# Five pieces of work moved in a two-network transformer kernel: attention's start, two spectra, GpSimd work, and a late norm factor

## The chip, the cores and the metric

The kernel runs on one core of one Trainium2 chip. Its engines each execute their own list of instructions in order: TensorE (PE, with its weight loads PEld) multiplies, VectorE (DVE), ScalarE (ACT) and GpSimd (POOL) work on elements, and SyncE (SP) issues the loads of weights. They wait for one another by semaphores. The metric is the device time of one launch in microseconds (us); three launches of the kernel before took 2412.6, 2415.0 and 2419.7 us.

## The reference

Two stacked blocks act on 256 latent rows, the second one also on 256 context rows, all of width 1024 and in float32. What matters here is the second block, in two layers:

```python
def na_hyena_mixer(h_lat, h_ctx, ...):           # layer 0
    # 8 heads of attention, latent queries on latent (with a bias) and context keys
    a_lat = merge_heads(neighbourhood_attention(qk_norm(qa_l), qk_norm(ka_l), va_l, k_c, va_c, rpb))
    b_lat = hyena_operator(p_lat[..., 3 * NA_WIDTH:], conv_w, conv_b, filter_params, d_bias)
    o_lat = jnp.concatenate([a_lat, b_lat], axis=-1) @ w_out
    ...                                          # the same for the context rows
def hyena_operator(u, conv_w, conv_b, filter_params, d_bias):
    x0, x1, v = jnp.split(short_conv(u, conv_w, conv_b), 3, axis=-1)
    z = v * x1
    y = long_conv(z, filt) + z * d_bias          # long_conv: product of spectra
    return y * x0
def modulate_2(x, gain, shift, scale):
    return rms_norm(x, gain) * (1 + scale) + shift
def swiglu_2(h, w_in, w_out):
    a, b = jnp.split(h @ w_in, 2, axis=-1)
    return (jax.nn.silu(a) * b) @ w_out
```

Layer 1 has a retention mixer in the place of attention: four heads whose score matrices are multiplied by decay tables, sums of exp(log gamma x distance) for the forward and the backward scan. Every mixer and every network takes a modulated norm of the residual, and adds its gated output to it.

## The kernel before

Activations lie with the channel on the partitions: `r` is the residual (8 tiles of 128 channels, 256 latent columns and 256 context columns), `yH` and `yL` its modulated norm as a high and a low part. Each product is three matmuls of reduced-precision floats (`mm3`, L172 high x high, L173 low activation x high weight, L174 high x low weight; in the changed file these are L175 to L177). Weights come in tiles `wraw` of 128x1024 by SP, in four buffers; `cut` makes the high part `wH` by a cast on ACT (L149) and the low part `wL` by a subtraction on DVE (L150), or on POOL for the hyena weights `even_hy`. There are three buffers of each. Matmul results lie in four groups of PSUM banks, `mm`, `sc`, `tp` and `sm`, two banks each.

The order of instructions on each engine is set by a scheduler from the order of the program and its own costs, and is then fixed: an instruction that waits holds back all that stand behind it on its engine.

Five places matter.

1. The mixer of layer 0 first makes q, k and v (`proj_tm`), then the generator `attention()` and the convolutions `conv(n)` run interleaved; `seg` 1 stands for the context queries. The softmax scale of a tile is L984 on DVE, PE then transposes the scaled tile (`tp`, L574).
2. `spectrum(s)` transforms `z` by matmuls (L585), multiplies it by the filter's spectrum (L1062 to L1074), and `signal(s, Y)` transforms it back (L1083, `mm` banks). `spectrum(0)` stands behind the first of the last four convolutions; `spectrum(1)` is in `rest()`, which runs in pieces between the tiles of the output product `even_out`.
3. The retention mixer's tables `decL` and `decC`: exponentials on ACT (L1310, L1311), then 24 instructions of 128x384 on DVE (L1313 to L1316). The `sg` buffers, two of them, hold the intermediate exponentials and are also used by `turn_y` (L1182).
4. The class `Norm` collects squares of the residual tile by tile (`add`), makes the factor 1/rms (`finish`: L329 and L330 sum over channels, L332 a root on ACT, L334 to L340 on DVE, L343 spreads it), and `modulated` writes `yH` and `yL` (L357 to L359).
5. The last network `fb1` (`up`, L425 on) starts after `flush()`, which issues all that is left of `modulated`.

Of the kernel before, what the change touches and what calls it, by code (L numbers as in the profile page):

```python
# [27 lines left out]
NEARLY = 9  # L28
LEADS = (1, 1, 0, 0)
# [44 lines left out]
def trace(tc, A, dbg=None):  # L74
# [50 lines left out]
    yH = tl(const, [P, ND, 2 * T], F32R, "yH")  # L125
    yL = tl(const, [P, ND, 2 * T], F32R, "yL")
# [26 lines left out]
    class Feed:  # L153
# [4 lines left out]
        def next(self):  # L158
            out = ready.pop((self.w, self.i), None) or cut(load(A[self.w][self.i]), self.eng)
            self.i += 1  # L160
            return out
# [200 lines left out]

    class TwoNorms(Norm):
# [91 lines left out]
    def ffn_steps(hp, nslot, w_gu, w_dn, keys, gate_ch, segs, norms, lead=0, done=None, pre=None):  # L455
# [29 lines left out]
        for gi, (k0, k1) in enumerate(groups):  # L485
            last = gi == len(groups) - 1
            fs = list(range(k0, k1))
            if gi == 0 and lead:
                for f in fs[:lead]:
                    hidden(f)  # L490
                for i, q in enumerate(segs):
                    if i:
                        flush()
                    for f in fs[:lead]:
                        ups(f, [q])
                        tick(-(-ND // lead))
                        yield
                fs = fs[lead:]
            for f in fs:
                hidden(f)  # L500
                ups(f, segs[:1] if f in pre else segs)
                yield
            for q in segs:
                need(keys[q], gate_ch)
            for part in ([[q] for q in segs] if last else [segs]):
                feed = Feed(w_dn, k0)
                for d in range(ND):
                    ps = bank(tags[d % 2], [P, T * len(part)])
                    down(ps, feed, k0, k1, part)
                    resid_add(ps, d, part, keys, gate_ch, norms if last else None)  # L510
                    tick(1)
                    yield
                if last and done is not None:
                    flush()
                    for q in part:
                        done(q)

    def ffn(w_gu, w_dn, keys, gate_ch, segs, to, norms, done=None, lead=0, start=0.0, by=1.0, hook=None, pre=None,
            nslot=0):
        both = len(segs) == 2  # L520
        with ExitStack() as st:
            hp = pool("ffn_h", stack=st)
            steps = ffn_steps(hp, nslot or (12 if both or w_dn in GROUPED else 22), w_gu, w_dn, keys, gate_ch, segs, norms, lead, done, pre)
# [379 lines left out]
    with ExitStack() as st:  # L903
# [9 lines left out]
        lat, ctx_ = (0, 1), (2, 3)  # L913
        for i, (n, tiles) in enumerate(((0, lat), (1, lat), (0, ctx_), (1, ctx_), (2, ctx_), (2, lat))):
            out = proj_tm("even_qkv", n, tiles, ("mm", "mm") if i % 2 == 0 else ("sc", "sc"))
            tick(4)
            for ps, tt in zip(out, tiles):
                if n == 2:
                    act.copy(vt[:, tt, :], ps)
                    continue  # L920
                sq = tl(tpool, [P, 512], F32, "sg", 2)
                act.activation(sq, ps, AF.Square)
                ss = tl(spool, [P, 8], F32, "qss")
                vec.tensor_reduce(ss, sq.rearrange("p (h e) -> p h e", h=8), AX, OP.add)
                rs = mean_rsqrt(ss, 8, 64)
                vec.tensor_tensor(qkn[n][:, tt, :].rearrange("p (h e) -> p h e", h=8),
                                  ps.rearrange("p (h e) -> p h e", h=8),
                                  rs.rearrange("p (h o) -> p h o", o=1).to_broadcast([P, 8, 64]), op=OP.mult)

# [31 lines left out]
        def weights(h, seg):  # L961
# [4 lines left out]
            for qt in (2 * seg, 2 * seg + 1):  # L966
# [17 lines left out]
                vec.tensor_scalar(s[:, :nk], s[:, :nk], rin, None, op0=OP.mult)  # L984
# [47 lines left out]

        def conv(n, dst):
# [13 lines left out]
        def spectrum(s):  # L1047
# [19 lines left out]
            vec.tensor_tensor(zr, zr, specB, op=OP.mult)  # L1067
            for i in range(2):
                vec.tensor_tensor(zi[i], zi[i], specA[:, i, :], op=OP.mult)
                vec.tensor_tensor(zi[i], zi[i], zr[:, i, :], op=OP.add)  # L1070
# [26 lines left out]
        steps = attention()  # L1097
# [5 lines left out]
        run(steps, 1)  # L1103
        hyx0 = tl(mp, [P, 4, 512], F32, "qk2n0", 1)
        for c in range(4):
            conv(c, hyx0[:, c, :])
            if c == 0:
                Y = spectrum(0)
        run(steps, 100)
        signal(0, Y)  # L1110
        heads(0)

        def rest():

            Y = spectrum(1)
            yield
            heads(1)
            yield
            signal(1, Y)
            yield  # L1120
# [18 lines left out]
    with ExitStack() as st:  # L1139
# [162 lines left out]
        for dst, pairs in ((DL, (0, 4)), (DC, (2,))):  # L1302
# [5 lines left out]
            for h in range(4):  # L1308
# [3 lines left out]
                if len(tabs) == 2:  # L1312
                    vec.tensor_tensor(ef, ef, tabs[1][:, 0, :], op=OP.mult)  # L1313
                    vec.tensor_tensor(dst[:, h, :], dst[:, h, :], tabs[1][:, 1, :], op=OP.mult)
                vec.tensor_tensor(dst[:, h, :], dst[:, h, :], ef, op=OP.add)
                vec.tensor_scalar(dst[:, h, :], dst[:, h, :], 1.0 / 16.0, None, op0=OP.mult)  # L1316
# [20 lines left out]
        nm = [Norm(0)]  # L1337
# [3 lines left out]
    flush()  # L1341
    ffn("fb1_gu", "fb1_dn", kk1, 8, [0], len(units), None)
# [172 lines left out]
```

## Time and profile before

| | |
|---|---|
| three launches | 2412.6, 2415.0, 2419.7 us |
| the profiled launch | 2415.01 us, of which the span of its instructions is 2413.3 us |
| PE busy | 2367.9 us (98%) |
| DVE busy | 1730.2 us (72%) |
| ACT busy | 1029.8 us (43%) |
| POOL busy | 47.4 us (2%) |
| mean granted TensorE clock | 0.993 |

PE is busy nearly everywhere, so the time it is idle, or runs at a lower clock, is what a change of order can take away or add. Of a row of a timeline the first number is the start, the second the duration; a bracket behind it has the idle time of the engine just before and what ended it. In the table of stretches each stretch has its length, then busy time of PE, PEld, DVE, ACT and POOL with the number of instructions, the granted clock and the share of the DMA engines.

### The profile page before, as it was taken

What the parts mean: (1) busy time and instruction counts of PE and PEld (TensorE: products, weight loads), DVE (VectorE), ACT (ScalarE), POOL (GpSimd) and SP (SyncE); (2) the same over time, 40 slices, a digit from 0 to 9 for tenths busy, and PEclk for the clock granted to TensorE, in tenths of its full rate; (3) what the DMA queues carried; (4) which work ended last, traced back from release to release, by engine and by line L of the source; (5) the groups of instructions that cost most, each with busy time, mean ns of one, the idle gap of its engine ahead of it and who ended that gap; (6) DMA issues with size and microseconds to landing.
All of it is one profiled execution on the core that took longest, in us unless ns stands there. A gap on an engine that the chain in (4) does not pass through costs nothing.

```text
span 2413.3 us, 38351 instructions
## 1 busy us (share of the span) xinstructions
PE 2367.9 (98%) x15304; PEld 2127.8 (88%) x15304; DVE 1730.2 (72%) x3063; ACT 1029.8 (43%) x1549; POOL 47.4 (2%) x47
## 2 busy tenths in 40 slices
PE   7999999999999999998999999999999999999999
PEld 4999889999998888877988888998888988999999
DVE  6889987665998689789875556877454786565554
ACT  4444575444432236675632222542222563344442
POOL 0000000000000000230000000000000000000000
PEclk9999999999999999999999999999999999999999
DMA  8897865665674455411463434564444542244554
GB/s 317 318 311 249 310 219 170 207 214 207 226 243 170 151 192 195 157 62 55 158 218 131 157 140 149 175 210 175 175 175 165 186 154 96 97 135 147 193 186 145
DMA packets 124660, 442.75 MB, mean 183 GB/s; under 512 B 13984, under 2 KB 18208, under 8 KB 124352
## 3 DMA queue, kind: packets, MB, share of 16 engines
q1 hardware_dynamic: 123216, 436.30, 51.9%
q0 software_dynamic: 1120, 3.80, 0.5%
q8 instruction: 120, 1.97, 0.3%
q14 instruction: 60, 0.49, 0.1%
q10 hardware_dynamic: 144, 0.19, 0.0%
HBM read 439.19 MB, written 1.05 MB: 182 GB/s over the span
## 4 chain that ended last, share of the span: by engine, by line
PE 53%; DVE 2%; ACT 1%; issue 0%; ACTq 0%
PE mm L172 9%; PE mm L173 9%; PE mm L174 9%; PE sc L174 8%; PE sc L172 8%; PE sc L173 8%; PE tp L1227 1%; PE sm L172 1%; PE sm L173 1%; PE sm L174 1%; PE tp L574 1%; PE mm L1083 0%; ACT wH L149 0%; DVE wL L150 0%; PE sm L1008 0%
## 5 line engine op out<-in xcount | busy, mean ns | idle before, releaser
L149 ACT CAST wH<-wraw 128x1024 fp32r<-128x1024 f32 x598 | 626.3, 1049 | 1036.6 <-PE mm L173 374.6
L150 DVE TENSOR_TENSOR wL<-wraw,wH 128x1024 fp32r<-128x1024 f32 x586 | 716.2, 1224 | 346.5 <-ACT wH L149 336.5
L172 PE MATMUL mm<-yH,wH 128*128 128x256 f32 (+1 forms) x1736 | 553.4, 319 | 6.4 <-ACT wH L149 3.8
L174 PE MATMUL mm<-yH,wL 128*128 128x256 f32 (+1 forms) x1736 | 551.0, 317 | 3.5 <-DVE wL L150 3.5
L173 PE MATMUL mm<-yL,wH 128*128 128x256 f32 (+1 forms) x1736 | 551.5, 318 | 0.6 <-DVE yL L702 0.3
L174 PE MATMUL sc<-yH,wL 128*128 128x256 f32 (+1 forms) x1192 | 385.9, 324 | 5.7 <-DVE wL L150 5.5
L172 PE MATMUL sc<-yH,wH 128*128 128x256 f32 (+1 forms) x1192 | 387.0, 325 | 0.4 <-ACT wH L149 0.3
L173 PE MATMUL sc<-yL,wH 128*128 128x256 f32 (+1 forms) x1192 | 385.2, 323 | 0.0
L172 PEld LDWEIGHTS mm<-yH,wH 128*128 128x128 f32 x1736 | 328.7, 189 | 29.8 <-ACT wH L149 4.1
L174 PEld LDWEIGHTS mm<-yH,wL 128*128 128x128 f32 x1736 | 328.5, 189 | 26.7 <-DVE wL L150 4.2
L173 PEld LDWEIGHTS mm<-yL,wH 128*128 128x128 f32 x1736 | 328.5, 189 | 23.4 <-DVE yL L702 1.0
L270 DVE SCALAR_TENSOR_TENSOR mjunk<-mraw,crow_c 128x1024 bf16<-128x1024 f32 x200 | 244.2, 1221 | 26.6 <-DMA mraw<-in_wada_dram 15.2
L174 PEld LDWEIGHTS sc<-yH,wL 128*128 128x128 f32 x1192 | 225.5, 189 | 26.6 <-DVE wL L150 7.2
L172 PEld LDWEIGHTS sc<-yH,wH 128*128 128x128 f32 x1192 | 225.8, 189 | 20.8 <-ACT wH L149 1.0
L173 PEld LDWEIGHTS sc<-yL,wH 128*128 128x128 f32 x1192 | 225.6, 189 | 20.1 <-DVE yL L178 0.5
L174 PE MATMUL sc<-hH,wL 128*128 128x256 f32 (+1 forms) x636 | 191.9, 302 | 1.2 <-DVE wL L150 1.2
L172 PE MATMUL mm<-hH,wH 128*128 128x256 f32 (+1 forms) x636 | 192.9, 303 | 0.0
L173 PE MATMUL mm<-hL,wH 128*128 128x256 f32 (+1 forms) x636 | 192.4, 303 | 0.0
L172 PE MATMUL sc<-hH,wH 128*128 128x256 f32 (+1 forms) x636 | 192.2, 302 | 0.0
L174 PE MATMUL mm<-hH,wL 128*128 128x256 f32 (+1 forms) x636 | 191.9, 302 | 0.0
L173 PE MATMUL sc<-hL,wH 128*128 128x256 f32 (+1 forms) x636 | 191.8, 302 | 0.0
L270 DVE SCALAR_TENSOR_TENSOR mjunk<-mraw,crow_c_ctx 128x1024 bf16<-128x1024 f32 x112 | 137.0, 1223 | 4.5 <-ACT crow_c_ctx L224 2.5
(418 smaller groups left out, 3289.5 us busy)
## 6 DMA issues: line engine op xcount, KB each, us to landing
mraw<-in_wmod_dram SPq DMA_DIRECT2D x144, 512.0 KB, 4.6
wraw<-in_fa_gu_dram SPq DMA_DIRECT2D x116, 512.0 KB, 3.6
wraw<-in_fb_gu_dram SPq DMA_DIRECT2D x94, 512.0 KB, 3.3
wraw<-in_w_gu_dram SPq DMA_DIRECT2D x88, 512.0 KB, 4.0
wraw<-in_fa_dn_dram SPq DMA_DIRECT2D x60, 512.0 KB, 3.7
mraw<-in_wada_dram SPq DMA_DIRECT2D x56, 512.0 KB, 5.4
wraw<-in_fb_dn_dram SPq DMA_DIRECT2D x52, 512.0 KB, 3.3
wraw<-in_w_dn_dram SPq DMA_DIRECT2D x44, 512.0 KB, 3.4
```

Of the source, the lines that this page charges most:

```text
L149: act.copy(H, raw)
L150: (eng or vec).tensor_tensor(L, raw, f32(H), op=OP.subtract)
L172: pe.matmul(ps, aH, bH, start=start, stop=False)
L173: pe.matmul(ps, aH, bL, start=False, stop=False)
L174: pe.matmul(ps, aL, bH, start=False, stop=stop)
L270: queued(vec.scalar_tensor_tensor(junk, raw, 1.0, row_of(c), op0=OP.mult, op1=OP.mult, accum_out=mod[key][:, ch * 8 + j:ch * 8 + j + 1]), ...
L574: pe.transpose(pt[:, j * P:j * P + P], src(j), ident)
L1227: pe.matmul(ps[:, c], kT[:, j, jt * P:jt * P + P], qT[:, j, :], start=j == 0, stop=j == 1)
```

## The change

Five parts. (1) `attention()` is created ahead of the loop over q, k, v, and its first steps run behind the context's value projection and behind the last one. (2) The softmax scale of the context queries goes to POOL (16 instructions of 128x256). (3) `spectrum(1)` follows the third of the last four convolutions, with attention finished ahead of it; three of its products (one of 128x1024, two of 128x512) go to POOL, and so do the subtractions of every second weight tile of `even_out` (8 of them). (4) The 24 instructions of the decay tables go to POOL. (5) `LateNorm` writes the residual times its gain, without 1/rms, into the unused context half of `yH` and `yL`, with the shift as two further columns; the first two hidden tiles of `fb1` are computed from it with 258 columns, multiplied by 1/rms afterwards, and the shift's product is added as a bias; `flush()` comes behind them.

```diff
+NLATE = 2
...
         def next(self):
-            out = ready.pop((self.w, self.i), None) or cut(load(A[self.w][self.i]), self.eng)
+            eng = nc.gpsimd if self.w == "even_out" and self.i % 2 else self.eng
+            out = ready.pop((self.w, self.i), None) or cut(load(A[self.w][self.i]), eng)
...
+    class LateNorm(Norm):
+        def __init__(self, key, which):
+            super().__init__(0)
+            self.a8 = modA[key][:, which * 8:which * 8 + 8]
+            sh = mod[key][:, which * 24:which * 24 + 8]
+            for i in range(2):
+                split(yHx[:, :, 2 * T + i], yLx[:, :, 2 * T + i], sh)
+        def add(self, d):
+            super().add(d)
+            c = slice(T, 2 * T)
+            a = self.a8[:, d:d + 1]
+            act.activation(yH[:, d, c], r[:, d, :T], AF.Identity, scale=a)
+            vec.scalar_tensor_tensor(yL[:, d, c], r[:, d, :T], a, f32(yH[:, d, c]), op0=OP.mult, op1=OP.subtract)
+        def finish(self):
+            super().finish()
+            self.rs = tl(tpool, [P, T], F32, "sqacc", 2)
+            act.copy(self.rs, self.rb)
+        def up(self, w_gu, f, hH, hL):
+            feed = Feed(w_gu, 2 * f)
+            W = [feed.next() for _ in range(2)]
+            ps = [bank(t) for t in ("mm", "sc")]
+            c = slice(T, 2 * T + 2)
+            both = [(k, i) for k in range(ND) for i in range(2)]
+            for k, i in both if f == 0 else sorted(both, key=lambda x: x[1]):
+                w = slice(k * P, k * P + P)
+                mm3(ps[i][:, :T + 2], W[i][0][:, w], W[i][1][:, w], yHx[:, k, c], yLx[:, k, c],
+                    k == 0, k == ND - 1)
+            b = tl(spool, [P, 2], F32, "ln_b")
+            x = []
+            for i in range(2):
+                act.copy(b[:, i:i + 1], ps[i][:, T:T + 1])
+                x.append(tl(tpool, [P, T], F32, "sq", 4))
+                vec.tensor_tensor(x[i], ps[i][:, :T], self.rs, op=OP.mult)
+            sg = tl(tpool, [P, 512], F32, "sg", 2)[:, :T]
+            act.activation(sg, x[0], AF.Silu, bias=b[:, 0:1])
+            h = tl(tpool, [P, 512], F32, "hf", 2)[:, :T]
+            vec.scalar_tensor_tensor(h, x[1], b[:, 1:2], sg, op0=OP.add, op1=OP.mult)
+            split(hH, hL, h)
...
-                ups(f, segs[:1] if f in pre else segs)
+                if late is not None and f < NLATE:
+                    late.up(w_gu, f, *hs[f]["all"])
+                    if f == NLATE - 1:
+                        flush()
+                else:
+                    ups(f, segs[:1] if f in pre else segs)
...
-                vec.tensor_scalar(s[:, :nk], s[:, :nk], rin, None, op0=OP.mult)
+                (nc.gpsimd if seg else vec).tensor_scalar(s[:, :nk], s[:, :nk], rin, None, op0=OP.mult)
...
+        steps = attention()
         for i, (n, tiles) in enumerate(((0, lat), (1, lat), (0, ctx_), (1, ctx_), (2, ctx_), (2, lat))):
             out = proj_tm("even_qkv", n, tiles, ("mm", "mm") if i % 2 == 0 else ("sc", "sc"))
             tick(4)
+            if i == 4:
+                run(steps, 2)
...
+        run(steps, 1)
...
-            vec.tensor_tensor(zr, zr, specB, op=OP.mult)
+            eng = nc.gpsimd if s else vec
+            eng.tensor_tensor(zr, zr, specB, op=OP.mult)
             for i in range(2):
-                vec.tensor_tensor(zi[i], zi[i], specA[:, i, :], op=OP.mult)
+                eng.tensor_tensor(zi[i], zi[i], specA[:, i, :], op=OP.mult)
...
-        run(steps, 1)
         hyx0 = tl(mp, [P, 4, 512], F32, "qk2n0", 1)
+        Y = {}
         for c in range(4):
             conv(c, hyx0[:, c, :])
             if c == 0:
-                Y = spectrum(0)
-        run(steps, 100)
-        signal(0, Y)
+                Y[0] = spectrum(0)
+            if c == 2:
+                run(steps, 100)
+                Y[1] = spectrum(1)
+        signal(0, Y[0])
...
                 if len(tabs) == 2:
-                    vec.tensor_tensor(ef, ef, tabs[1][:, 0, :], op=OP.mult)
-                    vec.tensor_tensor(dst[:, h, :], dst[:, h, :], tabs[1][:, 1, :], op=OP.mult)
-                vec.tensor_tensor(dst[:, h, :], dst[:, h, :], ef, op=OP.add)
-                vec.tensor_scalar(dst[:, h, :], dst[:, h, :], 1.0 / 16.0, None, op0=OP.mult)
+                    nc.gpsimd.tensor_tensor(ef, ef, tabs[1][:, 0, :], op=OP.mult)
+                    nc.gpsimd.tensor_tensor(dst[:, h, :], dst[:, h, :], tabs[1][:, 1, :], op=OP.mult)
+                nc.gpsimd.tensor_tensor(dst[:, h, :], dst[:, h, :], ef, op=OP.add)
+                nc.gpsimd.tensor_scalar(dst[:, h, :], dst[:, h, :], 1.0 / 16.0, None, op0=OP.mult)
...
-        nm = [Norm(0)]
+        nm = [LateNorm("l1", 2)]
...
-    flush()
-    ffn("fb1_gu", "fb1_dn", kk1, 8, [0], len(units), None)
+    ffn("fb1_gu", "fb1_dn", kk1, 8, [0], len(units), None, late=nm[0])
```

The order on ACT at the decay tables before: `sg`, `decL` and `decC` are the exponentials, `kT` the copy of a k projection, `wH` the casts of the next weight tiles of the k projection.

```order
980 L1310 ACT_TABLE_LOAD
981 L1310 ACTIVATE sg<-kT,lg 128x384
982 L1311 ACTIVATE decL<-kT,lg 128x384
983 L1310 ACTIVATE sg<-kT,lg 128x384
984 L1311 ACTIVATE decL<-kT,lg 128x384 x3
985 L1311 ACTIVATE decC<-kT,lg 128x384 x3
986 L1310 ACTIVATE sg<-kT,lg 128x384
987 L1311 ACTIVATE decC<-kT,lg 128x384
988 L1310 ACTIVATE sg<-kT,lg 128x384
989 L1172 COPY kT<-mm 128x256
990 L149 CAST wH<-wraw 128x1024 x2
991 L1310 ACTIVATE sg<-kT,lg 128x384 x4
```

The same place on ACT in the changed kernel:

```order
988 L1370 ACTIVATE decL<-kT,lg 128x384 x2
989 L1370 ACTIVATE decC<-kT,lg 128x384
990 L1369 ACTIVATE sg<-kT,lg 128x384 x2
991 L1370 ACTIVATE decC<-kT,lg 128x384 x2
992 L1369 ACTIVATE sg<-kT,lg 128x384 x2
993 L1370 ACTIVATE decC<-kT,lg 128x384
994 L1369 ACTIVATE sg<-kT,lg 128x384
995 L1231 COPY kT<-mm 128x256
996 L151 CAST wH<-wraw 128x1024 x3
```

The copy and the casts stood between the fourth and the fifth of the eight `sg`; now they stand behind the eighth.

DVE at the same place, before (`wL` at 2106 is the low part of the third tile of k weights):

```order
2102 L1315 TENSOR_TENSOR decC<-decC,sg 128x384 x2
2103 L1316 TENSOR_SCALAR decC<-decC 128x384 x2
2104 L1315 TENSOR_TENSOR decC<-decC,sg 128x384 x2
2105 L1316 TENSOR_SCALAR decC<-decC 128x384 x2
2106 L150 TENSOR_TENSOR wL<-wraw,wH 128x1024
```

DVE in the changed kernel, with the two instructions of `turn_y` (L1241), each of which takes an `sg` buffer that a POOL sum of the tables (L1374) has to give back:

```order
2065 L1213 TENSOR_TENSOR qT<-sq 128x256
2066 L1241 TENSOR_TENSOR sg<-yH,yL 128x512
2067 L1210 TENSOR_TENSOR sq<-mm,arope 128x256
2068 L1241 TENSOR_TENSOR sg<-yH,yL 128x512
2069 L152 TENSOR_TENSOR wL<-wraw,wH 128x1024 x3
```

The tables have left DVE, and two `turn_y` instructions stand ahead of the same `wL`; before, `turn_y` stood behind it.

DVE at the start of the last network, before (`hn` and `yL` are `modulated`, the last row is the network's third weight tile on):

```order
2340 L340 SCALAR_TENSOR_TENSOR nm_rs<-nm_t,nm_rs 128x2
2341 L357 SCALAR_TENSOR_TENSOR hn<-resid,moda_l_93,sm 128x256 x3
2342 L359 SCALAR_TENSOR_TENSOR yL<-hn,mod_l_92,yH 128x256 x3
2343 L357 SCALAR_TENSOR_TENSOR hn<-resid,moda_l_93,sm 128x256 x3
2344 L359 SCALAR_TENSOR_TENSOR yL<-hn,mod_l_92,yH 128x256 x3
2345 L357 SCALAR_TENSOR_TENSOR hn<-resid,moda_l_93,sm 128x256 x2
2346 L359 SCALAR_TENSOR_TENSOR yL<-hn,mod_l_92,yH 128x256 x2
2347 L150 TENSOR_TENSOR wL<-wraw,wH 128x1024 x2
```

DVE in the changed kernel, the end of that stretch (L405 and L409 are `LateNorm.up`; the `wL` of row 2328 is that of the network's fifth weight tile, the first of hidden tile 2):

```order
2322 L360 SCALAR_TENSOR_TENSOR hn<-resid,moda_l_93,sm 128x256 x2
2323 L405 TENSOR_TENSOR sq<-sc,sqacc 128x256
2324 L362 SCALAR_TENSOR_TENSOR yL<-hn,mod_l_92,yH 128x256
2325 L409 SCALAR_TENSOR_TENSOR hf<-sq,ln_b,sg 128x256
2326 L362 SCALAR_TENSOR_TENSOR yL<-hn,mod_l_92,yH 128x256 x2
2327 L360 SCALAR_TENSOR_TENSOR hn<-resid,moda_l_93,sm 128x256
2328 L152 TENSOR_TENSOR wL<-wraw,wH 128x1024
2329 L181 TENSOR_TENSOR hL<-hf,hH 128x256
2330 L362 SCALAR_TENSOR_TENSOR yL<-hn,mod_l_92,yH 128x256
2331 L152 TENSOR_TENSOR wL<-wraw,wH 128x1024 x4
```

The fifth tile's `wL` stands behind the scaling of hidden tile 1's second half (row 2323), which needs the last matmul of that tile.

## Rows read from the trace of the kernel before

**Rows 1.** The page's first part: busy time of each engine.

```profile
PE 2367.9 (98%) x15304; PEld 2127.8 (88%) x15304; DVE 1730.2 (72%) x3063; ACT 1029.8 (43%) x1549; POOL 47.4 (2%) x47
```

**Rows 2.** The table of stretches, its head and four stretches.

```profile
core 0: us, PE busy (x) PEld busy (x) DVE busy (x) ACT busy (x) POOL busy (x), PEclk, DMA share, GB/s
...
1010.00:1120.00 110.00, 103.45 (x537) 79.25 (x536) 99.74 (x209) 77.45 (x177) 32.38 (x27) 1.00 0.18 63
1140.00:1150.00 10.00, 5.78 (x28) 4.97 (x27) 10.00 (x18) 2.83 (x4) 0.00 (x0) 0.67 0.01 2
...
2216.00:2222.00 6.00, 4.57 (x19) 4.16 (x20) 4.61 (x13) 2.62 (x6) 0.00 (x0) 0.50 0.21 79
...
1970.00:1975.00 5.00, 2.66 (x8) 1.84 (x7) 5.00 (x12) 1.86 (x4) 0.00 (x0) 0.79 0.15 40
```

**Rows 3.** Groups of instructions by line, POOL alone: busy us, mean ns.

```profile
L150 POOL TENSOR_TENSOR wL<-wraw,wH 128x1024 fp32r<-128x1024 f32 x12 | 28.8, 2397 | 77.9 <-ACT wH L149 77.9
...
L998 POOL TENSOR_TENSOR vv<-v,vv 128x256 fp32r<-128x256 f32 x8 | 5.9, 742 | 13.1 <-ACT vv L997 12.4 <-PE tp L574 0.7
L744 POOL TENSOR_SCALAR_AFFINE_SELECT wst<-wst 128x1024 f32<-128x1024 f32 x1 | 1.1, 1087 | 9.2 <-DMA wst<-in_wsT_dram 9.2
...
masks.py:199 POOL TENSOR_SCALAR_AFFINE_SELECT ident<-ident 128x128 f32<-128x128 f32 x1 | 0.3, 292 | 0.1
```

**Rows 4.** Groups by line on DVE from 1955 to 1975 us, the decay tables.

```profile
L1315 DVE TENSOR_TENSOR decL<-decL,sg 128x384 f32<-128x384 f32 x4 | 2.2, 556 | 0.0
...
L1316 DVE TENSOR_SCALAR decL<-decL 128x384 f32<-128x384 f32 x4 | 1.4, 356 | 0.0
```

**Rows 5.** Timeline of ACT, the first exponential of the tables.

```profile
1959.77 0.62 ACT L1310 ACTIVATE sg<-kT,lg 128x384 f32<-128x384 f32 x1 [1.61 <-DVE lg L1297]
```

**Rows 6.** Timeline of DVE at the tables' end, and `turn_y`.

```profile
1971.35 0.63 DVE L1316 TENSOR_SCALAR decC<-decC 128x384 f32<-128x384 f32 x2
1971.88 1.23 DVE L150 TENSOR_TENSOR wL<-wraw,wH 128x1024 fp32r<-128x1024 f32 x1
...
1975.82 0.70 DVE L1182 TENSOR_TENSOR sg<-yH,yL 128x512 f32<-128x512 f32 x1
```

**Rows 7.** Timeline of PE at the tables' end.

```profile
1973.16 0.80 PE L174 MATMUL sc<-yH,wL 128*128 128x512 f32 x1 [2.34 <-DVE wL L150]
```

**Rows 8.** PE's waits from 960 to 1160 us: total, times, longest.

```profile
PE mm L1083 <- DVE a2pL L1071: 3.7, 1, 3.7
PE sm L1008 <- DVE a2pL L178: 1.6, 1, 1.6
```

**Rows 9.** Groups by line on DVE from 960 to 1150 us, the softmax scale.

```profile
L984 DVE TENSOR_SCALAR a2s<-a2s,sm_rin 128x256 f32<-128x256 f32 x16 | 7.7, 491 | 0.2
```

**Rows 10.** Timeline of DVE, two softmax scales of one shape.

```profile
1017.53 0.34 DVE L984 TENSOR_SCALAR a2s<-a2s,sm_rin 128x256 f32<-128x256 f32 x1
...
1020.03 1.09 DVE L984 TENSOR_SCALAR a2s<-a2s,sm_rin 128x256 f32<-128x256 f32 x1
```

**Rows 11.** Timeline of POOL at the same time.

```profile
1018.58 2.39 POOL L150 TENSOR_TENSOR wL<-wraw,wH 128x1024 fp32r<-128x1024 f32 x1 [3.10 <-ACT wH L149]
```

**Rows 12.** Timeline of DVE, the products of `spectrum(1)`, beginning and end.

```profile
1136.53 1.23 DVE L1062 TENSOR_TENSOR a2pH<-a2pL,specA 128x1024 f32<-128x1024 f32 x1 [0.30 <-PE mm L585]
...
1145.42 0.69 DVE L1072 TENSOR_TENSOR a2pL<-a2pH 128x512 f32<-128x512 f32 x1
```

**Rows 13.** Timeline of PE at the start of the last network.

```profile
2212.14 0.28 PE L174 MATMUL sc<-mH,wL 128*128 128x256 f32 x1
...
2218.63 0.58 PE L172 MATMUL mm<-yH,wH 128*128 128x256 f32 x1 [1.11 <-ACT yH L358]
...
2222.14 0.27 PE L172 MATMUL sc<-yH,wH 128*128 128x256 f32 x1
2222.26 0.28 PE L173 MATMUL sc<-yL,wH 128*128 128x256 f32 x1
```

**Rows 14.** Timeline of DVE there, three of the eight columns of `modulated`.

```profile
2217.55 1.27 DVE L357 SCALAR_TENSOR_TENSOR hn<-resid,moda_l,sm 128x256 f32<-128x256 f32 x3 [1.38 <-PE sm L343]
```

More of the change, by code (lines that the diff above doesn't have):

```diff
@@ L124, in trace @@
     r = tl(const, [P, ND, 2 * T], F32, "resid")
-    yH = tl(const, [P, ND, 2 * T], F32R, "yH")
-    yL = tl(const, [P, ND, 2 * T], F32R, "yL")
+    yHx = tl(const, [P, ND, 2 * T + 2], F32R, "yH")
+    yLx = tl(const, [P, ND, 2 * T + 2], F32R, "yL")
+    yH, yL = yHx[:, :, :2 * T], yLx[:, :, :2 * T]
     last_load = [None]
@@ L453, in ahead, with ffn_steps @@
             yield
-    def ffn_steps(hp, nslot, w_gu, w_dn, keys, gate_ch, segs, norms, lead=0, done=None, pre=None):
+    def ffn_steps(hp, nslot, w_gu, w_dn, keys, gate_ch, segs, norms, lead=0, done=None, pre=None, late=None):
         N = T * len(segs)
@@ L518, in ffn @@
     def ffn(w_gu, w_dn, keys, gate_ch, segs, to, norms, done=None, lead=0, start=0.0, by=1.0, hook=None, pre=None,
-            nslot=0):
+            nslot=0, late=None):
         both = len(segs) == 2
@@ L522, in ffn @@
             hp = pool("ffn_h", stack=st)
-            steps = ffn_steps(hp, nslot or (12 if both or w_dn in GROUPED else 22), w_gu, w_dn, keys, gate_ch, segs, norms, lead, done, pre)
+            steps = ffn_steps(hp, nslot or (12 if both or w_dn in GROUPED else 22), w_gu, w_dn, keys, gate_ch, segs, norms, lead, done, pre, late)
             n = NF + ND * (len(GROUPS) if both or w_dn in GROUPED else 1) + (lead + ND if both else 0)
@@ L912, in trace @@
         pos = tl(mp, [P, 4, 512], F32, "at2")
[L913 to L928, printed above, removed]
         qg8 = tl(mp, [P, 1], F32, "qg8")
@@ L1031, in attention @@
                 yield
+        steps = attention()
+        lat, ctx_ = (0, 1), (2, 3)
+        for i, (n, tiles) in enumerate(((0, lat), (1, lat), (0, ctx_), (1, ctx_), (2, ctx_), (2, lat))):
+            out = proj_tm("even_qkv", n, tiles, ("mm", "mm") if i % 2 == 0 else ("sc", "sc"))
+            tick(4)
+            if i == 4:
+                run(steps, 2)
+            for ps, tt in zip(out, tiles):
+                if n == 2:
+                    act.copy(vt[:, tt, :], ps)
+                    continue
+                sq = tl(tpool, [P, 512], F32, "sg", 2)
+                act.activation(sq, ps, AF.Square)
+                ss = tl(spool, [P, 8], F32, "qss")
+                vec.tensor_reduce(ss, sq.rearrange("p (h e) -> p h e", h=8), AX, OP.add)
+                rs = mean_rsqrt(ss, 8, 64)
+                vec.tensor_tensor(qkn[n][:, tt, :].rearrange("p (h e) -> p h e", h=8),
+                                  ps.rearrange("p (h e) -> p h e", h=8),
+                                  rs.rearrange("p (h o) -> p h o", o=1).to_broadcast([P, 8, 64]), op=OP.mult)
+        run(steps, 1)
         def conv(n, dst):
@@ L1096, in trace @@
         hyfeed = Feed("even_hy", 0, nc.gpsimd)
-        steps = attention()
         for c in range(4):
@@ L1107, in trace @@
             if c == 0:
-                Y = spectrum(0)
-        run(steps, 100)
-        signal(0, Y)
+                Y[0] = spectrum(0)
[3 more added lines that the diff above has]
+        signal(0, Y[0])
         heads(0)
         def rest():
-            Y = spectrum(1)
-            yield
             heads(1)
             yield
-            signal(1, Y)
+            signal(1, Y[1])
             yield
```

## The prediction

> **What bounds the kernel now.** I read the page's busy times first: PE is busy 98% of the span, so the other 45 us and the stretches at a lower clock are all that a new order can give back, and anything that makes PE wait elsewhere adds in full [rows 1]. Then the table of stretches, to find where these 45 us lie; the change touches four of the places. In the convolutions of layer 0 (1010 to 1120 us) PE idles 110.00 - 103.45 = 6.55 us while DVE is busy 99.74 of 110 us [rows 2]. Behind them, from 1140 to 1150 us, PE idles 4.22 us at a granted clock of 0.67, and DVE is busy all of it [rows 2]. At the retention tables PE has one wait of 2.34 us [rows 7]. Between the last two networks nothing but the norm runs: the last matmul starts at 2212.14 us, the next real one at 2218.63, and the clock is then 0.50, which is the lower level, until about 2222 [rows 2, 13]. Last I read the waits and timelines there, to see which instruction each wait ends with, and set the orders of both kernels beside them. The profiled launch took 2415.01 us, which is also the median of the three; I add to that number.
>
> **The decay tables, the largest term.** All 24 instructions leave DVE, which took 0.556 us for one with two inputs and 0.356 us for the scale [rows 4]. POOL shows no 128x384, but two sizes with two inputs: 742 ns at 256 columns and 2397 ns at 1024 [rows 3]. The line through them gives 0.742 + 128 x 1.655/768 = 1.02 us at 384. For one input the nearest rows are the two selections, 292 ns at 128 and 1087 ns at 1024 [rows 3]; their line gives 0.52 us at 384. What waits for POOL is told by the order: two `turn_y` instructions on DVE take an `sg` buffer each, which the sums of the last two tables give back, and they stand ahead of the `wL` for which PE waited before. Up to the last of these sums POOL has 16 instructions of two inputs and 7 scales: 16 x 1.02 + 7 x 0.52 = 19.9 us. It starts with the first exponential, which ended at 1959.77 + 0.62 = 1960.4 us [rows 5], so it is there at 1980.3; a `turn_y` adds 0.70 [rows 6] and the `wL` 1.23, which makes 1982.2 us in the place of 1971.88 + 1.23 = 1973.1 [rows 6]. PE waited until 1973.16 for this `wL` [rows 7], so it stands 9.1 us longer. ACT doesn't help it: the casts of these tiles now stand behind the eighth exponential, which waits for the sixth sum in its turn. Nothing else stands in PE's list there, and the stages behind are PE's own, so that no later slack gives it back. After the 2.34 us the stretch showed a clock of 0.79 [rows 2]; I add 0.4 us for a longer idle time: **+9.5 us**. Bounds: were POOL as fast as DVE, 16 x 0.556 + 7 x 0.356 = 11.4 us end at 1971.8 and the `wL` at 1973.7, +0.6; were its scale as slow as a sum of two, 23 x 1.02 = 23.5 us give +12.7, and with waits for DVE in between some +14. I take the lines through POOL's own rows.
>
> **The convolutions of layer 0.** DVE loses 16 scales of 491 ns, 7.7 us [rows 9], and the early start of attention moves some of its work ahead of 1010 us. POOL takes the scales at 0.292 + 128 x 0.795/896 = 0.41 us each [rows 3], 6.5 us in about 100, but in its list they stand between weight cuts of 2.4 us and must wait for DVE's reciprocals. Of the 6.55 us of idle PE [rows 2] I take 4 back; bounds 0 and 6.5, plus a loss of 2 if a scale is late behind a cut.
>
> **The second spectrum.** Before, the products ran on DVE from 1136.53 to 1146.1 us [rows 12] and PE waited 3.7 us for them [rows 8], then went on at the lower clock; the 5.78 us busy at 0.67 would have been 3.9 at full clock, so the stretch cost 4.2 + 1.8 = 6 us [rows 2]. Now the last convolution stands behind the four transforms. That gives cover for the products: 24 matmuls of 512 columns at about 0.235 us and some 49 of 256 columns at 0.12 us [rows 13], with the first signal's 16 short ones about 13 us, against a chain of 9.6 us plus what POOL adds, 2.40 + 2 x 1.30 - 1.23 - 2 x 0.69 = +2.4 us if DVE waits for all of it. So the old wait goes. New ones come: the four transforms stand back to back in PE's list with two `mm` banks, which conv 2 has just filled; the second pair waits for DVE's two subtractions of the first, the last convolution for those of the second, and the first signal's second bank for the evictions behind them. Each of these is one or two DVE instructions of 0.69 us [rows 12] behind an ACT copy, 1.2 to 1.9 us, and there are four of them: 5 us, bounds 2 and 8. The tail gives 6 - 5 = 1 us (-2 to +4). With the convolutions: **-5 us**, between -10 and +4. The odd `even_out` cuts on POOL cost nothing: one in two tiles means 2.4 us in 48 x 0.12 = 5.8 us of PE time; without that cover it would be 8 x (2.40 - 1.22) = 9 us.
>
> **The late norm.** PE now goes from the mixer's last matmul into hidden tiles 0 and 1 without the norm: 96 matmuls at 0.12 us [rows 13], from 2212.3 (with some norm matmuls between) to about 2225. But in DVE's list the `wL` of the next weight tile stands behind all of `LateNorm.up` for both tiles, and seven of the eight columns of `modulated`. The scaling of tile 1's second half can't start before the last of the 96 matmuls; behind it come seven instructions of 0.42 us [rows 14] and the `wL` of 1.23: 2225.4 + 0.5 + 2.9 + 1.2 = 2230 us. PE stops for 4 to 5 us there, and then goes some 3.5 us at the lower clock, as it did before from 2218.63 to 2222.14 [rows 13]. Counting matmuls: before, the 116th began at about 2222.1 + 101 x 0.12 = 2234.2; now it begins 20 behind the restart at about 0.21 each, 2230 + 4.2 = 2234.2. **0 us**: the wait for the factor has become a wait for a weight. If that `wL` is in time, the gain is 2218.63 - 2212.3 plus 1.7 us of slow clock less norm matmuls, 6.8 us; at worst, with ACT's copies late, -2 becomes a loss of 2.
>
> **The sum.** 2415.0 + 9.5 - 5 + 0 = 2419.5 us, taken as **2419**.
>
> **A rule against the change.** A DVE scale of 128x256 that took 0.34 us alone took 1.09 when it began at 1020.03 us, inside a POOL cut of two inputs that ran from 1018.58 to 1020.97; it ended 0.15 us later [rows 10, 11]. So here one engine held the other up, at least for that form. The Trainium skill (SBUF — State Buffer, "Who interferes with whom") says why: the two share one pair of ports, a DVE instruction of two SBUF inputs or in a two-port mode and a GpSimd instruction that reads SBUF shut each other out for a whole instruction. By that rule, with which the two scales agree, moving work from DVE to POOL relieves DVE of nothing where both are wanted; the rival "no relief" below is its consequence.
>
> **Rivals.**
> - *No relief (slower).* Place: the convolutions and the second spectrum. Price: POOL's new 6.5 us of scales and 5.0 us of products are paid by DVE as waits, as in [rows 10], against 7.7 + 2.6 us taken from it. Then the 6.55 us stay, and the second spectrum's new waits eat its 6: mixer +1 instead of -5, with the tables +9.5: 2425.5. It decides if DVE's scales and products near POOL's work stretch by 0.5 us or more on the average. For it: the row of 1.09 us; against: with POOL cutting for 28.8 us in this stretch [rows 3], the mean of all sixteen, 491 ns, is only 0.15 above the short one [rows 9, 10].
> - *Cheap tables.* POOL does 384 columns at near DVE's price, or the `turn_y` wait ends on an earlier sum: +0.6 instead of +9.5, 2410.6. Against it: the 2397 ns of twelve cuts, which DVE does in 1222.
> - *All covers hold.* The network's `wL` is in time (-6.8), the mixer gives 10, and the tables cost 0.6 to 9.5: 2398.8 to 2407.7, say 2403. Against it: DVE's order at both places.
>
> **How the numbers follow.** A launch of this kernel can be told from no change beyond about 0.3%, 7.2 us: below 2407.8 is faster, above 2422.2 slower. The forecast, 2419 +- 5, has 0.42 (0.30 the same, 0.12 slower); no relief 0.20 (0.05 the same, 0.15 slower); cheap tables 0.18 (0.12 the same, 0.06 faster); all covers hold 0.20 (0.18 faster, 0.02 the same). So faster 0.24, same 0.49, slower 0.27. The range from 2402 to 2428 leaves out about half of the last rival and a tenth of the slower one; the forecast's own range is 2414 to 2424.
>
> **What would show it.** In the changed profile: POOL busy about 47 + 6.5 + 5 + 19 + 20.5 = 98 us, a 128x384 sum near 1.0 us and a scale near 0.5; one PE wait of 10 to 12 us for `wL` in the k projection; no wait of 3.7 us at L1143 but several of 1 to 2 us at L639 and in the last convolution; PE running into the last network without the 6 us gap and a wait for `wL` of 4 to 5 us some 13 us later. It is wrong if the tables cost under 4 us, if PE shows no wait for `wL` in the first 30 us of the last network, or if the mixer of layer 0 is not 1 to 9 us shorter.

## The result and the profile after

The changed kernel took 2440.9 us (median of 4 launches, 2438.3 to 2442.4) against 2417.3 for the kernel before on the same chips: a ratio of 1.0101, 95% interval 1.0089 to 1.0114. It is slower by 24 us, outside the predicted range of 2402 to 2428.

To see where, one instruction that both kernels have at the same point of the program serves as a mark: the last step of each norm's factor on DVE (`nm_rs`, L340 before, L343 after). The view of one line gives the starts of its first and last instance in a stretch; here the pair behind the first mixer, before and after:

```profile
L340 DVE SCALAR_TENSOR_TENSOR nm_rs<-nm_t,nm_rs x2: 160/160/160, 1170.9 to 1193.6; 128x2 f32<-128x2 f32 x2
```

```profile
L343 DVE SCALAR_TENSOR_TENSOR nm_rs<-nm_t,nm_rs x2: 161/161/161, 1178.9 to 1201.7; 128x2 f32<-128x2 f32 x2
```

From each pair the later start is taken. The differences of such marks, in us of the profiled launches (the last column runs to the end of the span):

| | to the first mark | first mixer | two networks | retention mixer | last network |
|---|---|---|---|---|---|
| before | 936.4 | 257.2 | 372.1 + 372.1 | 278.2 | 197.3 |
| after | 934.5 | 267.2 | 372.8 + 372.6 | 294.1 | 195.3 |

So the first mixer lost 10.0 us and the retention mixer 15.9; the last network gained 2.0, and the two networks that the change does not touch lost 1.2. In the profiles of all fourteen kernels the first mark lies between 931.6 and 941.4 us, so the 1.9 us ahead of it are not put down to the change.

**The retention mixer.** PE's longest waits over the whole span of the changed kernel, as totals, times and the longest:

```profile
PE sc L175 <- ACT wH L151: 15.9, 2, 13.1
PE sc L177 <- DVE wL L152: 8.4, 6, 4.3
```

The 13.1 and the 4.3 are here, in the place of the one wait of 2.34 in [rows 7]. POOL's instructions by line, with mean durations, answer to [rows 3]:

```profile
L1021 POOL TENSOR_SCALAR a2s<-a2s,sm_rin 128x256 f32<-128x256 f32 x16 | 15.0, 948 | 4.7 <-ACT a2s L1018 2.3 <-DVE sm_rin L1020 1.3 <-PE sm L1045 1.1
...
L1375 POOL TENSOR_SCALAR decC<-decC 128x384 f32<-128x384 f32 x4 | 5.7, 1417 | 0.3
L1375 POOL TENSOR_SCALAR decL<-decL 128x384 f32<-128x384 f32 x4 | 4.7, 1168 | 0.3
...
L1374 POOL TENSOR_TENSOR decC<-decC,sg 128x384 f32<-128x384 f32 x4 | 4.0, 994 | 0.2
```

The sum of two tables took 0.99 us, the predicted 1.02. The scale, with one input, took 1.17 at least, more than the sum, and not 0.52. How the chain ends, on POOL, DVE, ACT and PE in turn:

```profile
1994.60 0.99 POOL L1374 TENSOR_TENSOR decC<-decC,sg 128x384 f32<-128x384 f32 x1
```

```profile
1992.80 0.69 DVE L1241 TENSOR_TENSOR sg<-yH,yL 128x512 f32<-128x512 f32 x1 [20.55 <-POOL decC L1374]
...
1995.63 0.69 DVE L1241 TENSOR_TENSOR sg<-yH,yL 128x512 f32<-128x512 f32 x1 [1.80 <-POOL decC L1374]
1996.24 3.79 DVE L152 TENSOR_TENSOR wL<-wraw,wH 128x1024 fp32r<-128x1024 f32 x3
```

```profile
1990.47 0.61 ACT L1369 ACTIVATE sg<-kT,lg 128x384 f32<-128x384 f32 x1 [2.45 <-POOL decC L1374]
...
1991.24 2.94 ACT L151 CAST wH<-wraw 128x1024 fp32r<-128x1024 f32 x3
```

```profile
1992.34 0.79 PE L175 MATMUL sc<-yH,wH 128*128 128x512 f32 x1 [13.12 <-ACT wH L151]
1997.82 0.79 PE L177 MATMUL sc<-yH,wL 128*128 128x512 f32 x1 [4.26 <-DVE wL L152]
```

The order of waiting is the predicted one: POOL's last sum, `turn_y` on DVE, then `wL`, then PE. DVE stood idle 20.55 us ahead of the first `turn_y`, which waited for an `sg` buffer. ACT's casts came late too, behind the eighth exponential, but they were not last: `wL` was. Through the long idle time the clock fell to its lower level, as two stretches of the table show (columns as in [rows 2]):

```profile
1985.00:1990.00 5.00, 0.00 (x0) 0.00 (x0) 0.00 (x0) 1.74 (x3) 4.75 (x5) 0.50 0.00 0
...
1995.00:2000.00 5.00, 2.18 (x5) 1.80 (x6) 4.37 (x5) 0.00 (x0) 2.26 (x2) 0.50 0.22 78
```

**The first mixer.** A stall that was not there before lies where attention now starts, first PE's timeline, then the stretch:

```profile
991.44 0.80 PE L1007 MATMUL sc<-kH,qq 128*128 128x512 f32 x1 [2.53 <-ACT kH L993]
...
994.58 0.80 PE L175 MATMUL sc<-wH,yH 128*128 128x512 f32 x1 [1.07 <-ACT a2s L1013]
```

```profile
990.00:1000.00 10.00, 7.49 (x21) 5.51 (x22) 6.81 (x13) 7.51 (x13) 1.07 (x2) 0.66 0.27 91
```

The same place on PE in the kernel before, the transposes and the first scores:

```profile
1001.01 1.04 PE L947 MATMUL tp<-ident,qk2n 128*128 128x128 f32 x8
...
1004.69 0.40 PE L970 MATMUL sc<-kH,qq 128*128 128x512 f32 x1
```

Twelve matmuls of a convolution ran between the two, and the scores did not wait. In the changed kernel the first scores stand right behind the transposes of q and k in PE's list and wait for ACT to scale and split them; the matmuls behind wait for the bank that the scores fill. The second spectrum, on PE, on DVE and on POOL:

```profile
1122.50 1.10 PE L639 MATMUL mm<-a2pH,dft 128*128 128x512 f32 x2 [2.02 <-DVE qk2n L1103]
...
1126.28 3.78 PE L639 MATMUL mm<-a2pH,dft 128*128 128x512 f32 x4 [0.68 <-ACT hf L641]
...
1141.19 1.16 PE L1143 MATMUL mm<-dft,qk2n 128*128 128x128 f32 x8 [1.51 <-DVE sq L1147]
1144.13 2.02 PE L1143 MATMUL mm<-dft,qk2n 128*128 128x128 f32 x16 [1.79 <-DVE qk2n L1103]
```

```profile
1132.43 2.50 DVE L1124 TENSOR_TENSOR sg<-a2pL,specB 128x512 f32<-128x512 f32 x2
1134.86 3.48 DVE L1125 TENSOR_TENSOR a2pH<-a2pH,sg 128x512 f32<-128x512 f32 x2
```

```profile
1131.40 2.38 POOL L1127 TENSOR_TENSOR a2pL<-a2pL,specB 128x1024 f32<-128x1024 f32 x1 [7.49 <-DVE a2pH L1121]
1134.41 3.37 POOL L1129 TENSOR_TENSOR a2pL<-a2pL,specA 128x512 f32<-128x512 f32 x2 [0.63 <-DVE sg L1124]
```

The wait of 3.7 us in [rows 8] is gone, and waits of 1 to 2 us stand in its place, as predicted. DVE's pairs took 2.50 and 3.48 us beside POOL's products; the same pairs with POOL idle took 1.28 (run mix_dve, below).

**The last network.** PE ran into it without a gap, and then waited:

```profile
2253.08 0.38 PE L175 MATMUL sc<-yH,wH 128*128 128x256 f32 x1 [2.78 <-ACT wH L151]
2254.58 0.58 PE L177 MATMUL mm<-yH,wL 128*128 128x256 f32 x1 [1.00 <-DVE wL L152]
```

3.8 us of waiting in two pieces, for the cast and for the low part of the weight behind the late tiles; 4 to 5 were predicted. The prediction named the low part on DVE alone. The longer piece ended on ACT's cast, which stood behind a copy of the late tiles (`ln_b`) and three columns of `modulated` on ACT.

### The profile page after: what moved, and what is told of

It is laid out like the page before. It is cut to its first block, busy times and chain, and to the rows that moved or that the text cites. A ratio compares the mean times of both kernels' runs of the same rounds, so it can differ in the third digit from the quotient of the medians.

```text
span 2436.5 us, 38432 instructions
## 1 busy us (share of the span) xinstructions
PE 2370.3 (97%) x15304; PEld 2125.5 (87%) x15304; DVE 1723.7 (71%) x3026; ACT 1034.4 (42%) x1564; POOL 113.6 (5%) x98
## 4 chain that ended last, share of the span: by engine, by line
PE 77%; DVE 3%; ACT 1%; POOL 1%; issue 0%; ACTq 0%; DVEq 0%
PE mm L176 13%; PE mm L175 12%; PE mm L177 12%; PE sc L177 12%; PE sc L175 11%; PE sc L176 11%; PE sm L175 1%; PE sm L176 1%; PE sm L177 1%; PE tp L628 1%; PE tp L1286 1%; ACT wH L151 0%; DVE wL L152 0%; PE mm L639 0%; PE sm L1045 0%
## 5 line engine op out<-in xcount | busy, mean ns | idle before, releaser
L152 DVE TENSOR_TENSOR wL<-wraw,wH 128x1024 fp32r<-128x1024 f32 x578 | 706.5, 1224 | 342.1 <-ACT wH L151 333.0
L175 PE MATMUL mm<-yH,wH 128*128 128x256 f32 (+2 forms) x1736 | 552.9, 319 | 6.4 <-ACT wH L151 3.8
L177 PE MATMUL mm<-yH,wL 128*128 128x256 f32 (+2 forms) x1736 | 552.2, 318 | 4.7 <-DVE wL L152 4.7
L176 PE MATMUL mm<-yL,wH 128*128 128x256 f32 (+2 forms) x1736 | 551.9, 318 | 0.8 <-DVE yL L756 0.3
L175 PE MATMUL sc<-yH,wH 128*128 128x256 f32 (+2 forms) x1192 | 384.8, 323 | 16.0 <-ACT wH L151 15.9
L177 PE MATMUL sc<-yH,wL 128*128 128x256 f32 (+2 forms) x1192 | 386.2, 324 | 7.1 <-DVE wL L152 7.1
L176 PE MATMUL sc<-yL,wH 128*128 128x256 f32 (+2 forms) x1192 | 384.4, 322 | 0.0
```

Of the source, the lines that this page charges most:

```text
L152: (eng or vec).tensor_tensor(L, raw, f32(H), op=OP.subtract)
L175: pe.matmul(ps, aH, bH, start=start, stop=False)
L176: pe.matmul(ps, aH, bL, start=False, stop=False)
L177: pe.matmul(ps, aL, bH, start=False, stop=stop)
```

## The experiments

Each was timed 4 to 12 times; the kernel before, timed beside them, had a median of 2415.9 to 2417.3. Lengths of mixers and networks are by the marks above, in the profiled launch.

**tables_dve.** The tables back on DVE in the changed kernel:

```diff
-                nc.gpsimd.tensor_tensor(dst[:, h, :], dst[:, h, :], ef, op=OP.add)
+                vec.tensor_tensor(dst[:, h, :], dst[:, h, :], ef, op=OP.add)
...
```

> The changed kernel with the 24 instructions of the decay tables back on DVE, all else as changed. Theory (the tables on POOL and the exponentials, casts and low parts queued behind them cost the retention mixer the 15.9 us by which it grew): 2440.9 - 16 = 2425 us, one wait of about 2.3 us at the k projection. Rival (the mixer grew by what comes before it or by the late norm's extra work in its output product): no shorter than 2436.

Measured 2425.4 us, ratio to before 1.0032 (1.0021 to 1.0044): 15.5 us less than the changed kernel. The retention mixer is back at 278.6 us, 15.5 less too, with one wait of 2.3. The theory holds.

**tables_pool_only.** The reverse edit in the kernel before.

> The kernel before with only the decay tables moved to POOL. Theory: 2417.3 + 16 = 2433 us, with the same two waits for the cast (13 us) and for the low part (4 us) as in the changed kernel, and 128x384 scales on POOL of 1.17 us. Rival (the loss needs the other parts): within 4 us of 2417.

Measured 2433.8 us, ratio 1.0070 (1.0057 to 1.0082), the mixer 295.2 us. PE's waits there:

```profile
PE sc L172 <- ACT wH L149: 13.2, 1, 13.2
PE sc L174 <- DVE wL L150: 4.3, 1, 4.3
```

The tables alone make the retention mixer's loss: 17.0 us by the marks here, 15.5 in the changed kernel.

**mix_dve.** In the changed kernel, scales, products and cuts back on DVE:

```diff
-                (nc.gpsimd if seg else vec).tensor_scalar(s[:, :nk], s[:, :nk], rin, None, op0=OP.mult)
+                vec.tensor_scalar(s[:, :nk], s[:, :nk], rin, None, op0=OP.mult)
...
-            eng = nc.gpsimd if s else vec
+            eng = vec
...
-            eng = nc.gpsimd if self.w == "even_out" and self.i % 2 else self.eng
+            eng = self.eng
```

> The changed kernel with the softmax scales, the three spectrum products and the odd output cuts back on DVE; the new order of attention and spectra, the tables on POOL and the late norm stay. Theory A (the first mixer's 10 us are mostly the shared ports: POOL's products and DVE's stretched ones): 2440.9 - 5 to - 7 = 2434 to 2436 us, and DVE's pair of products L1124 back at 1.3 us from 2.5, its pair L1125 at 1.3 from 3.5. Theory B (they are the order: an early start that PE waits for, and four transforms in a row): no more than 2 us shorter, 2439 or more.

Measured 2443.7 us, ratio 1.0111 (1.0096 to 1.0126): 2.8 us more than the changed kernel, though DVE's pairs were back at 1.28 us. Theory A fell: the first mixer took 270.5 us, 3.3 more. Its loss is the order's, and POOL's work took some of it away.

**late_only.** The late norm alone in the kernel before.

> The kernel before with the late norm alone. Theory: the last network and its norm gain 2 us as in the changed kernel, 2417.3 - 2 = 2415 us, with PE running on at 2212 us and a wait of 2 to 4 us for a weight some 12 us later. Rival (all covers hold once the rest is undisturbed): -6.8, 2410.5.

Measured 2414.6 us, ratio 0.9991 (0.9982 to 0.9999), with waits of 2.7 and 1.0 us behind the late tiles. The covers do not hold by themselves. The gain of 2 us is not shown to be the last network's: that took 196.7 us, 0.6 less than before, while 2.1 us lie ahead of the first mark, and the two networks in the middle took 372.8 and 372.6.

**no_early.** Attention's start put back:

```diff
-            if i == 4:
-                run(steps, 2)
...
-        run(steps, 1)
...
+        run(steps, 1)
         hyx0 = tl(mp, [P, 4, 512], F32, "qk2n0", 1)
```

> The changed kernel with attention started where it was before (the generator's first step behind the convolutions of z); spectra, POOL's work, tables and late norm as changed. Theory (the order costs the first mixer its 10 us, about half of it at the early start, where PE stood idle 3.6 us around 990 us and then ran at the lower clock): 2440.9 - 5 = 2436 us, no wait for kH at L1007 near 990. Rival (the stall only moves, since the first steps of attention wait for the same chain wherever they stand): within 2 us of 2441.

Measured 2432.3 us, ratio 1.0062 (1.0049 to 1.0075): 8.6 us less than the changed kernel, more than the 5 expected; the first mixer took 258.7 us.

**no_spec.** The second spectrum back in the output product:

```diff
-            if c == 2:
-                run(steps, 100)
-                Y[1] = spectrum(1)
+        run(steps, 100)
...
+            Y[1] = spectrum(1)
+            yield
             heads(1)
```

> The changed kernel with the second spectrum back among the tiles of the output product and attention finished behind the last convolution, as before; its three products stay on POOL, so do the scales, the early start stays. Theory (the four transforms in a row, PE's waits from 1120 to 1150 us, cost about 5 us more than the wait they replaced): 2440.9 - 5 = 2436. Rival (the products on POOL, 2.4 us longer than on DVE, make the old wait of 3.7 us longer by as much): within 2 us of 2441.

Measured 2443.0 us, ratio 1.0106 (1.0093 to 1.0119). The rival was right about the time: with the early start in place, the spectrum's move neither made the loss nor cured it. Its mechanism went further than it said: the old wait, back in its place, was 8.6 us and not 3.7 + 2.4.

**no_early_no_spec.** Both edits.

> Both of the two moves undone: before's order of attention and spectra, with scales, products, odd output cuts and tables on POOL and the late norm. Theory (the order alone is the first mixer's loss, and POOL's relief is worth some 3 us in it): 2440.9 - 10 to - 13 = 2428 to 2431. Rival (POOL's work is a loss in the old order, through the shared ports): 2433 to 2436.

Measured 2432.4 us, ratio 1.0063 (1.0051 to 1.0075), first mixer 257.0 us: 8.5 us less than the changed kernel, between the two ranges and nearer the rival's. Here PE waits for the second spectrum's products longer than before:

```profile
PE mm L1139 <- DVE a2pL L1127: 7.3, 1, 7.3
```

The products on POOL account for 1.1 of the 3.6 us more (run products_only, below). Most of the rest falls to a weight cut of `even_out`, one of those that the change gave to POOL, beside DVE's pair of sums, which took 1.29 before; POOL first, then DVE:

```profile
1140.71 2.79 POOL L152 TENSOR_TENSOR wL<-wraw,wH 128x1024 fp32r<-128x1024 f32 x1
```

```profile
1141.21 3.43 DVE L1126 TENSOR_TENSOR a2pL<-a2pL 128x512 f32<-128x512 f32 x2
```

**early_only.** The early start alone in the kernel before.

> The kernel before with only attention's early start. Theory (the early steps make PE wait near 990 us, and use up the work that covered the first spectrum): +9 to +12, 2426 to 2429 us. Rival (it costs only together with POOL's work): within 3 us of 2417.

Measured 2427.2 us, ratio 1.0052 (1.0039 to 1.0065); the first mixer took 267.8 us, 10.6 more. PE's waits there, 935 to 1205 us:

```profile
PE mm L1088 <- DVE a2pL L1076: 5.0, 1, 5.0
PE sc L953 <- ACT kH L939: 2.5, 1, 2.5
PE mm L172 <- DVE qk2n L1049: 2.0, 1, 2.0
PE sc L172 <- ACT a2s L959: 1.9, 1, 1.9
PE sc L953 <- DVE qq L937: 1.5, 1, 1.5
PE mm L585 <- ACT qk2n L1065: 1.3, 1, 1.3
```

The 2.5 and the 1.9 are the stall at the start, and behind it the clock was 0.69 from 1000 to 1010 us. The 1.3 (the first spectrum's transforms) and the 2.0 (the convolution that follows) were not among the waits before, nor was any of that length at these lines, and the 5.0 was 3.7: attention's steps, run off earlier, no longer lie beside them.

**products_only.** The second spectrum's three products on POOL in the kernel before.

> The kernel before with only the second spectrum's three products on POOL. Theory (POOL's 2.4 and 1.3 us products and DVE's of two inputs beside them shut each other out, so the chain that PE waits for grows): the wait of 3.7 us at L1083 becomes 6 to 8, 2417.3 + 4 = 2421 us, with DVE's L1065 and L1066 longer than 1.3 us a pair. Rival (the chain is shared out between two engines and gets shorter): 2414.

Measured 2416.2 us, ratio 1.0005 (0.9996 to 1.0014). DVE's pairs stretched to 2.50 and 3.43 us, as the theory has it, but PE's wait only grew from 3.7 to 4.8: what DVE no longer computes paid for most of the stretching. The size was wrong, and the time came out for neither the theory nor the rival.

**fold.** The tables' 1/16 as a bias in the exponent, in the kernel before:

```diff
-                act.activation(ef, tabs[0][:, 0, :], AF.Exp, scale=lg[:, h:h + 1])
+                act.activation(ef, tabs[0][:, 0, :], AF.Exp, scale=lg[:, h:h + 1], bias=l16)
...
-                vec.tensor_scalar(dst[:, h, :], dst[:, h, :], 1.0 / 16.0, None, op0=OP.mult)
```

> The kernel before with the tables' factor 1/16 taken into the exponentials (a bias of ln(1/16) on ACT), so that the 8 scales of the tables go altogether; the other 16 instructions stay on DVE. Theory (the wait of 2.34 us and the 1.4 us at the lower clock behind it come from DVE's 24 instructions standing ahead of the weight's low part): 2416.4 - 3 = 2413. Rival (the wait is set by the exponentials on ACT and the two sg buffers): within 1 us.

Measured 2413.2 us, ratio 0.9986 (0.9978 to 0.9994); the retention mixer took 274.8 us, 3.4 less, and the wait of 2.34 is gone.

**scale_fold.** That, and the 16 scales of the context queries on POOL.

> The kernel before with the 16 softmax scales of the context queries on POOL, and the tables' 1/16 in the exponentials. Theory (the scales give back 3.8 of the 6.55 us in which PE waits between 1010 and 1120 us, the exponentials 3.4): 2417.3 - 7 = 2410 us. Rival (what the scales give is lost to the shared ports or later): -3.4 alone, 2414.

Measured 2409.4 us, ratio 0.9976 (0.9966 to 0.9987); the first mixer took 252.0 us, 5.2 less. PE's idle time in the convolutions fell from 6.55 us in [rows 2] to 2.63:

```profile
1010.00:1120.00 110.00, 107.37 (x560) 83.66 (x559) 95.26 (x201) 80.54 (x180) 48.86 (x44) 1.00 0.21 68
```

**scale_fold_late16.** With the late norm, and a row length of 528:

```diff
-    yHx = tl(const, [P, ND, 2 * T + 2], F32R, "yH")
+    yHx = tl(const, [P, ND, 2 * T + 16], F32R, "yH")
```

> The run scale_fold with the late norm, whose activations have rows of 528 columns in the place of 514. Theory (514 columns cost 0.6 us in each of the two networks between the mixers, by the alignment of a row; the late norm itself gains 2 us): those networks back at 372.1 us each, 2410 - 2 = 2408 us. Rival (the networks' 0.6 us have another cause): 372.7 again, 2409.

Measured 2401.3 us, ratio 0.9941 (0.9928 to 0.9953), faster than both kernels and than both forecasts. The two networks took 372.3 and 372.2 us, so most of the 0.6 us each came back; the last network took 195.0. The profiled launch is 9.4 us below that of scale_fold: 4.4 of them lie behind the first mark, the other 5.0 ahead of it (932.7 against 937.7 us), in a part of the program that no edit here is meant to touch. Whether those 5 us belong to the edit is not settled.

The length of a row as the cause of the 0.6 us is not shown either. Two groups of PE's matmuls in 360 us of the first of the two networks, in the kernel before, in late_only (514 columns) and here (528); `yH` has the longer rows, `hH` is the network's own hidden tile and has not:

```profile
L172 PE MATMUL mm<-yH,wH 128*128 128x512 f32 x152 | 60.0, 395 | 0.0
L172 PE MATMUL mm<-hH,wH 128*128 128x512 f32 x56 | 21.8, 389 | 0.0
```

```profile
L174 PE MATMUL mm<-yH,wH 128*128 128x512 f32 x152 | 59.8, 393 | 0.0
L174 PE MATMUL mm<-hH,wH 128*128 128x512 f32 x56 | 22.1, 394 | 0.0
```

```profile
L174 PE MATMUL mm<-yH,wH 128*128 128x512 f32 x152 | 59.7, 393 | 0.0
L174 PE MATMUL mm<-hH,wH 128*128 128x512 f32 x56 | 22.1, 395 | 0.0
```

The matmuls on the longer rows did not grow. Those on `hH` and `hL` did, with 514 columns and with 528: from one start to the next they add up to 122.8, 124.5 and 124.4 us in this network, those on `yH` and `yL` to 246.9, 246.0 and 245.3. Why the first grew, and why 528 columns make the second shorter still, no run here shows.

## Why the prediction was wrong

**The tables: the mechanism was right, a price was not.** The term was +9.5 us and measured 15.5 (tables_dve). Every wait of the chain was there, and the two-input price from the line through POOL's rows (1.02 us) held within 3%. The failed step is "For one input the nearest rows are the two selections ... 0.52 us at 384": the scale took 1.17 us with DVE idle, and up to 1.67 beside DVE. From the first instruction at 1969.80 to the end of the last sum at 1995.59 POOL needed 25.8 us and not 19.9; seven scales of 8.7 us in the place of 3.6 are 5.1 of the 5.9 us more. The upper bound (12.7 to 14) rested on the scale being no slower than a sum of two, which the rows did not say. PE's two waits, 17.4 us in the place of 2.34, are 15.0 longer, which is the 9.1 of the prediction and these 5.9. Of the 15.9 us by which the mixer grew some 0.9 are left; with the lower level still granted from 1995 to 2000 they are put down to the clock, for which 0.4 had been added.

**The early start was counted as a gain.** The early start of attention "moves some of its work ahead of 1010 us": that priced DVE's load and nothing else. The step that failed is that one: it asked what the move takes from the busy stretch, not what stands in PE's list where it puts the work. Before, twelve matmuls of a convolution stood between the transposes and the first scores. The edit puts the scores straight behind the transposes on which they rest. Alone it costs the first mixer 10.6 us (early_only), in the changed kernel 8.6 (no_early). In early_only about 4.4 us are idle time at the start; the clock behind it is some 2.6, an estimate from 0.69 over 10 us in which PE was busy 8.43; the rest are the later waits that attention's steps used to cover. That last part is read from the waits of two kernels and was not tried by itself. The prediction's own sign of being wrong, a first mixer not 1 to 9 us shorter, was met: it was 10.0 us longer.

**The scales on POOL did what was forecast.** 4 of the 6.55 us were to come back; 3.9 of them did in scale_fold, though a scale took 0.92 us and not 0.41: there POOL has room. The price is the same error as in the tables: POOL was busy 113.6 us in the changed kernel and not the 98 foreseen, and the two kinds of scale are 14.7 of the 15.6 us more. In the changed kernel the products and the odd cuts on POOL take this gain back: with the old order the first mixer took 257.0 us (no_early_no_spec), against 252.0 in scale_fold and 257.2 before.

**The second spectrum came out near zero, by the terms named.** Old wait gone, several waits of 1 to 2 us in its place (the old stretch cost 4.2 + 1.9 us by its own row, not 4.2 + 1.8, which changes nothing); the move is worth nothing in the time (no_early against no_early_no_spec, 2432.3 and 2432.4). By the marks the first mixer is 1.7 us longer for it with the old start of attention and 2.5 shorter with the early one (no_spec). The rival "no relief" was half right. Its mechanism is shown: DVE's pairs at 1.28 us took 2.50 and 3.48 beside POOL, and one took 3.43 beside a cut on POOL. But where it applied it lengthened PE's wait by 1.1 us (products_only), not by the price it was given, and the scales were relieved all the same. The odd cuts were called free because PE's time covers them; no_early_no_spec shows that they are not free to DVE, which is what PE waits for there. They were not run alone.

**The late norm came out near its forecast**, 0, with the wait for the next weight where the order put it. In the changed kernel the last network is 2.0 us shorter, in late_only 0.6, and its length varies by more than 1 us where its code is the same (197.3 in fold, 198.6 in scale_fold), so that a gain is not shown. What no step had are 0.5 to 0.8 us more in each of the two networks between the mixers, in every kernel here that has the late norm with 514 columns.

The sum, by the marks: tables +15.5, early start +8.5, the two networks +1.2 and the last network -2.0 make 23.2 of the 25.1 us by which the changed kernel is longer behind the first mark; the remaining 1.9 lie in the two mixers and have no run of their own.

## What to carry to other kernels

Before work is given to an engine that has done little of that kind, find a row of the very operation; a neighbour with as many inputs is not a bound. When a generator of steps is started earlier, read the list of the engine that bounds the kernel at the new place: a dependent chain with nothing between its links is a stall, and the old place loses its filling. A wait in front of one weight tile is cured more cheaply by taking instructions out of the queue ahead of it (here eight scales folded into exponents, 3.4 us) than by moving the queue to a slower engine.

## What the runs showed of the hardware

- On GpSimd a multiplication of one tensor by a scalar was slower than an instruction of two tensors: 0.92 us (scale_fold) against 0.74 for a subtraction at 128x256 [rows 3], 1.17 against 0.99 for a sum at 128x384.
- Two engines on elementwise work held each other up: DVE's pairs of two-input instructions of 128x512 took 2.50 to 3.48 us in place of 1.28 when POOL worked on two inputs beside them. The Trainium skill (SBUF — State Buffer, "Who interferes with whom") gives this as an exclusive lock on a shared pair of ports, and these rows agree.
- With two columns more in each row of `yH` and `yL` a network of 372.1 us took some 0.6 longer, with sixteen more 0.1 to 0.2. The matmuls that grew read other tensors, `hH` and `hL`: 394 to 395 ns on the average in place of 389, at 128x512. The cause is open.
